# The gate and up products of a hybrid decoder's feed-forward part, as seven half-size block products

## The chip, the cores and the metric

The program runs on one core of a Trainium2 chip, in one launch. The metric is the device time of that launch in microseconds. The engines are called by their names or by the profile's abbreviations: TensorE (PE; its weight loads PEld), VectorE (DVE), ScalarE (ACT), GpSimd (POOL) and SyncE (SP), whose queue issues the loads.

## The reference, cut to what matters

One inference step of a two-layer trunk, on 512 prompt positions and 8 x 4 decode positions, 544 columns in all, with a model width of 1024. Each layer has a mixing half (four head groups) and a feed-forward half. The change is in the feed-forward half:

```python
def hybrid_layer(x, pos, k_pos, st, p):
    ...
    x = x + jnp.concatenate([out_a, out_b, out_c, out_d], axis=-1) @ p['w_out']
    h2 = rmsnorm(x, p['norm2_g'])
    gate, f_conv_new = causal_dwconv(st['f_conv'], h2 @ p['ffn_w_gate'], p['ffn_conv_w'])
    x = x + (jax.nn.silu(gate) * (h2 @ p['ffn_w_up'])) @ p['ffn_w_down']
```

`causal_dwconv` is a causal depthwise convolution of width 3 over positions; the feed-forward width is 2816. All values are float32.

## The kernel before, in words

Channels lie on the partitions: an activation is a tile of 128 channels by 544 positions (`T`), in two halves of 272 (`HT`). The width 1024 is 8 such tiles (`NK`), the feed-forward width 2816 is 22 blocks of 128 (`NF`).

Every product is split in two: `split` (L496) and `xsplit` (L543) make a high part with ScalarE (a copy to fp32r) and a low part with VectorE (the difference). `gemm` (L654) then adds, for each of the k-blocks, the three terms high x high, high x low and low x high, each for both halves, in one PSUM tile. One matmul is 128 x 128 weights by 272 columns.

Weights come from a generator `weights()` (L604) in the order of use. `wload` loads one weight tile into the ring `wr` (two slots) through the SP queue; `wprep` (L633) makes its high part `wh` on ScalarE (L641) and its low part `wl` on VectorE (L643), in rings of three slots each; `wnext` keeps up to three ready and hands out the oldest.

The order of TensorE's instructions is the one in which the program emits them (class `Order` interleaves the side work of the mixing half by due times; the feed-forward half has no side work). The other engines' order is chosen by the framework's scheduler, by order of emission among what is ready.

The feed-forward half of a layer (L1555 to L1609) runs over `FGROUPS`, four groups of 6, 6, 6 and 4 blocks. For each block f of a group: `pgt` is the gate product; two VectorE instructions scale it by `rstd` into `pbf` (L1576, L1577); GpSimd copies the conv state in and out; `conv` (L692) is one ScalarE and two VectorE instructions (`cacc`); ScalarE applies SiLU (`sl`); GpSimd multiplies by `rstd` (L1584); VectorE multiplies by the up product `pup` (L1590) and `split` makes `hdh`, `hdl`. After a group's blocks come 8 down products `pdn` over that group's `hid`, each added to x by VectorE (L1600). The last group of the last layer ends in `finale` (L550, `pdl`), which works half by half. The right-hand sides `xs` of the gate and up products are splits of x times g without `rstd`; `rstd` is made by `Norm.finish` (L526), whose matmuls (`nps`) stand inside the first up product.

PSUM: ring `mm` of two wide tiles (gate, up, down), ring `ps` of two, and the single tiles `pa0` and `pa1`.

## Time and profile before

| what | us |
|---|---|
| median of 3 runs | 1375.87 (1374.64 to 1376.35) |
| the profiled execution | 1375.83 |
| its span, first to last instruction | 1374.0 |
| TensorE busy | 1343.9 |
| VectorE busy | 777.2 |
| ScalarE busy | 515.2 |
| GpSimd busy | 292.2 |

The span is what the profile covers; 1.8 us of the profiled execution's time lie around it. Busy times overlap. The feed-forward half of layer 0 begins at 285.35 us of the span, that of layer 1 at 963.72.

### The profile page before, as it was taken

What the parts mean: (1) busy time and instruction counts of PE and PEld (TensorE: products, weight loads), DVE (VectorE), ACT (ScalarE), POOL (GpSimd) and SP (SyncE); (2) the same over time, 40 slices, a digit from 0 to 9 for tenths busy, and PEclk for the clock granted to TensorE, in tenths of its full rate; (3) what the DMA queues carried; (4) which work ended last, traced back from release to release, by engine and by line L of the source; (5) the groups of instructions that cost most, each with busy time, mean ns of one, the idle gap of its engine ahead of it and who ended that gap; (6) DMA issues with size and microseconds to landing.
All of it is one profiled execution on the core that took longest, in us unless ns stands there. A gap on an engine that the chain in (4) does not pass through costs nothing.

```text
span 1374.0 us, 30046 instructions
## 1 busy us (share of the span) xinstructions
PE 1343.9 (98%) x12982; PEld 1299.8 (95%) x12982; DVE 777.2 (57%) x1319; ACT 515.2 (37%) x852; POOL 292.2 (21%) x466
## 2 busy tenths in 40 slices
PE   8899999999999999999998999999999999999997
PEld 7888888999999999999998888989999999999997
DVE  5897944665445445435658977537444444444446
ACT  5446324443223223313534353335432332232234
POOL 2431220032103102203124311202320230121121
PEclk9899999999999999999999999999999999999999
DMA  6222241232232232232432222413223232322323
GB/s 224 89 83 72 82 133 43 82 113 77 81 106 79 76 107 80 74 106 67 140 120 79 78 82 62 138 52 87 92 81 89 93 85 80 98 89 71 103 68 96
DMA packets 48084, 125.62 MB, mean 91 GB/s; under 512 B 10144, under 2 KB 14432, under 8 KB 47824
## 3 DMA queue, kind: packets, MB, share of 16 engines
q1 hardware_dynamic: 47952, 123.70, 29.6%
q8 instruction: 102, 1.67, 0.5%
q14 instruction: 30, 0.25, 0.1%
HBM read 115.01 MB, written 8.67 MB: 90 GB/s over the span
## 4 chain that ended last, share of the span: by engine, by line
PE 88%; DVE 8%; issue 2%; ACT 1%; DMA 0%; DVEq 0%; SPq 0%; ACTq 0%
PE pup L417 19%; PE pgt L417 19%; PE pdn L417 19%; PE po L417 7%; PE ptm L417 2%; PE pj_b L417 2%; PE pj_z L417 2%; PE pj_u L417 2%; PE pj_h L417 2%; PE pj_cq L417 2%; PE pj_c L417 2%; PE p L417 2%; PE pj_v L417 1%; DVE wl L643 1%; DVE cacc L696 1%
## 5 line engine op out<-in xcount | busy, mean ns | idle before, releaser
L641 ACT ACTIVATE wh<-wr 128x1024 fp32r<-128x1024 f32 (+3 forms) x218 | 208.5, 957 | 502.0 <-PE pdn L417 177.2
L643 DVE TENSOR_TENSOR wl<-wr,wh 128x1024 fp32r<-128x1024 f32 (+3 forms) x218 | 246.2, 1129 | 24.2 <-ACT wh L641 18.3
L417 PE MATMUL pgt<-xl,wh 128*128 128x272 f32 x704 | 146.7, 290 | 0.0
L417 PE MATMUL pup<-xl,wh 128*128 128x272 f32 x704 | 146.7, 290 | 0.0
L417 PE MATMUL pup<-xh,wl 128*128 128x272 f32 x704 | 145.9, 289 | 0.0
L417 PE MATMUL pgt<-xh,wl 128*128 128x272 f32 x704 | 145.9, 289 | 0.0
L417 PE MATMUL pup<-xh,wh 128*128 128x272 f32 x704 | 145.9, 288 | 0.0
L417 PE MATMUL pgt<-xh,wh 128*128 128x272 f32 x704 | 145.9, 288 | 0.0
L417 PE MATMUL pdn<-hdl,wh 128*128 128x272 f32 x688 | 142.8, 289 | 0.0
L417 PE MATMUL pdn<-hdh,wh 128*128 128x272 f32 x688 | 142.4, 288 | 0.0
L417 PE MATMUL pdn<-hdh,wl 128*128 128x272 f32 x688 | 142.2, 288 | 0.0
L1600 DVE TENSOR_TENSOR xr<-xr,pdn 128x544 f32<-128x544 f32 x62 | 44.7, 721 | 142.0 <-PE pdn L417 141.8
L1578 POOL COPY sfo<-pbf 128x2 f32<-128x2 f32 x44 | 14.8, 336 | 517.9 <-DVE pbf L1576 517.9
L1576 DVE TENSOR_TENSOR pbf<-pgt,rstd 128x512 f32<-128x512 f32 x44 | 30.5, 693 | 148.3 <-PE pgt L417 142.9
L417 PEld LDWEIGHTS pgt<-xh,wh 128*128 128x128 f32 x704 | 110.8, 188 | 0.0
L417 PEld LDWEIGHTS pup<-xh,wh 128*128 128x128 f32 x704 | 110.8, 188 | 0.0
L417 PEld LDWEIGHTS pup<-xl,wh 128*128 128x128 f32 x704 | 110.7, 189 | 0.0
L417 PEld LDWEIGHTS pgt<-xl,wh 128*128 128x128 f32 x704 | 110.7, 189 | 0.0
L417 PEld LDWEIGHTS pgt<-xh,wl 128*128 128x128 f32 x704 | 110.7, 188 | 0.0
L417 PEld LDWEIGHTS pup<-xh,wl 128*128 128x128 f32 x704 | 110.7, 188 | 0.0
L417 PEld LDWEIGHTS pdn<-hdl,wh 128*128 128x128 f32 x688 | 108.1, 188 | 0.1
L417 PEld LDWEIGHTS pdn<-hdh,wl 128*128 128x128 f32 x688 | 108.1, 188 | 0.0
(523 smaller groups left out, 2680.0 us busy)
## 6 DMA issues: line engine op xcount, KB each, us to landing
wr<-w_g SPq DMA_DIRECT2D x44, 512.0 KB
wr<-w_u SPq DMA_DIRECT2D x44, 512.0 KB
wr<-w_ch SPq DMA_DIRECT2D x38, 512.0 KB
wr<-w_d SPq DMA_DIRECT2D x48, 384.0 KB
wr<-w_o SPq DMA_DIRECT2D x12, 384.0 KB
wr<-w_d SPq DMA_DIRECT2D x16, 256.0 KB
xr<-x_in SPq DMA_DIRECT2D x7, 544.0 KB
wr<-w_tm SPq DMA_DIRECT2D x8, 392.0 KB
```

The costliest lines, as they stand in the source:

```text
L417: nc.tensor.matmul(out, lhsT, rhs, **kw)
L641: act(hi, r, AF.Copy)
L643: tt(lo, r, hi.bitcast(F32), op=ALU.subtract)
L696: stt(acc[:, 0:out_n], pb[:, j:j + out_n], wcol[:, j:j + 1], acc[:, 0:out_n], op0=ALU.mult, op1=ALU.add)
L1576: tt(pb[:, 2:2 + SEQ], pflat(p, 0, SEQ), rstd[:, 0:SEQ], op=ALU.mult)
L1578: pool.tensor_copy(sfo[:, f, 0:2], pb[:, SEQ:SEQ + 2])
L1600: tt(xk(m), xk(m), pflat(p), op=ALU.add)
```

## The change

For 19 of the 22 blocks the gate and the up product are taken together as one 2 x 2 block product: the weights are [g1 g2; u1 u2], with 1 and 2 for the first and second four k-blocks, the right-hand side is h = x g rstd with its two k-halves (1, 2) and two column halves. Seven products of half size, with sums of weights and of right-hand sides, give the four results.

- `FGROUPS` becomes five groups of 3, 5, 5, 5 and 4 blocks. The first three blocks (`PLAIN`) stay as they were. `FFN_ORDER` puts the 8 down products of a group between the blocks of the next one, two (in the last group three, three and two) after each block but the last; the last group's own stand at the end.
- `Forms.make` makes the right-hand sides, for one pair of k-blocks each time: two scalings by g and `rstd`, four sums, and the high and low parts of seven half-wide forms. It is called twice after block 0 and twice after block 1.
- `wload` puts gate and up weights of such a block in one buffer (`wgu`, one slot, two DMAs); `wsums` makes two more weight tiles on VectorE (`s31` holds g1 + u1 and u2 + u1 in its halves; `s24` holds g1 + u1 + u2 and g2 + g1 + u1 + u2); `wprep` splits g, s31, s24 and the second half of u.
- `seven` runs the seven chains of 12 matmuls over three PSUM tiles `pA`, `pB`, `pD` and one of the ring `mm` (`pC`), with four copies out of PSUM by ScalarE (`sn`) between chains that go on in the same tile, and VectorE sums for gate and up. The chains use, in this order, g, g, s31, s24, s24, s31, u. No product with `rstd` is left on GpSimd in these blocks.
- The squares' sums of the second norm move from GpSimd to VectorE (`Norm((dve, dve))`).
- Several SBUF pools become one (`slabs`, 51 slots), and a scratch area for DMA is made smaller.

```diff
-FGROUPS = [(0, 6), (6, 12), (12, 18), (18, 22)]
+FGROUPS = [(0, 3), (3, 8), (8, 13), (13, 18), (18, 22)]
+PLAIN = 3
...
+def _ffn_order():
+    o, todo = [], []
+    for f0, f1 in FGROUPS:
+        n = f1 - f0
+        for j, f in enumerate(range(f0, f1)):
+            o.append(("plain" if f < PLAIN else "seven", f, f0, f1))
+            k = -(-len(todo) // max(n - 1 - j, 1))
+            o += todo[:k]
+            todo = todo[k:]
+        o += todo
+        todo = [("down", m, f0, f1) for m in range(NK)]
+    return o + todo
...
+    slabs = ctx.enter_context(tc.tile_pool(name="slabs", bufs=51))
     wrp = ctx.enter_context(tc.tile_pool(name="wrp", bufs=2))
+    wgu = ctx.enter_context(tc.tile_pool(name="wgu", bufs=1))
+    wsp = ctx.enter_context(tc.tile_pool(name="wsp", bufs=2))
     whp = ctx.enter_context(tc.tile_pool(name="whp", bufs=3))
     wlp = ctx.enter_context(tc.tile_pool(name="wlp", bufs=3))
...
-                pool.tensor_tensor(a, a, b, op=ALU.add)
+                self.es[0].tensor_tensor(a, a, b, op=ALU.add)
...
+    class Forms:
+        def __init__(self, src):
+            self.src, self.got, self.b11 = src, [], None
+
+        def make(self, kp):
+            h = []
+            for k in (kp, kp + NK // 2):
+                x, g = self.src(k)
+                t = n5("hn", T)
+                stt(t, x, g, rstd, op0=ALU.mult, op1=ALU.mult)
+                h.append(t)
+            (b11, b12), (b21, b22) = ((t[:, 0:HT], t[:, HT:T]) for t in h)
+            u, v = n5("fu", T), n5("fv", T)
+            n1, n2, t3, n4 = u[:, 0:HT], u[:, HT:T], v[:, 0:HT], v[:, HT:T]
+            tt(n1, b11, b12, op=ALU.subtract)
+            stt(n2, n1, -1.0, b22, op0=ALU.mult, op1=ALU.subtract)
+            tt(t3, b22, b12, op=ALU.subtract)
+            tt(n4, b21, n2, op=ALU.add)
+            j = kp % 2
+            if j == 0:
+                self.b11 = [nx("f1" + c, [128, T], F32R) for c in "hl"]
+            c_ = slice(HT * j, HT * j + HT)
+            act(self.b11[0][:, c_], b11, AF.Copy)
+            tt(self.b11[1][:, c_], b11, self.b11[0][:, c_].bitcast(F32), op=ALU.subtract)
+            sb, su, sv = split(h[1], "f2"), split(u, "f3"), split(v, "f4")
...
+    def chain(o, wt, k0, xs, start=True):
+        hi, lo = wt
+        n = len(xs)
+        for k in range(n):
+            xh, xl = xs[k]
+            for i, (w, x) in enumerate(((hi, xh), (hi, xl), (lo, xh))):
+                mm(o, w[:, k0 + k, :], x, start=start and k == 0 and i == 0, stop=k == n - 1 and i == 2,
+                   skip_group_check=not start)
+            yield 0.0
...
+    def wsums(gu):
+        K = NK // 2
+        g, u = gu[:, 0], gu[:, 1]
+        s31 = wsp.tile([128, NK, 128], F32, tag="ws", name="s31")
+        s24 = wsp.tile([128, NK, 128], F32, tag="ws", name="s24")
+        q = gu.rearrange("p a (h k) f -> p (a h) (k f)", h=2)
+        tt(s31.rearrange("p (h k) f -> p h (k f)", h=2), q[:, 0:4:3], bc(q[:, 2], 1, 2), op=ALU.add)
+        tt(s24[:, 0:K], g[:, 0:K], s31[:, K:NK], op=ALU.add)
+        tt(s24[:, K:NK], g[:, K:NK], s24[:, 0:K], op=ALU.add)
+        return [g, s31, s24, u[:, K:NK]]
...
-            nrm = Norm((pool, pool))
+            nrm = Norm((dve, dve))
...
+            def seven(f):
+                B11, B21, B22, N1, N2, T3, N4 = fm.parts()
+                K = NK // 2
+                a_ = ps("pA", [128, HT])
+                b_ = psa.tile([128, HT], F32, tag="pa1", name="pB")
+                d_ = psa.tile([128, HT], F32, tag="pa0", name="pD")
+                sn = pd.tile([128, 4, HT], F32, tag="d5", name="sn")
+                pb, dec = gate_in(f)
+                n = SEQ - HT
+                wg_ = wnext()
+                yield from chain(a_, wg_, 0, B11)
+                act(sn[:, 0], a_, AF.Copy)
+                yield from chain(b_, wg_, K, B21)
+                tt(pb[:, 2:2 + HT], b_, sn[:, 0], op=ALU.add)
+                w31 = wnext()
+                yield from chain(d_, w31, K, N1)
+                act(sn[:, 1], d_, AF.Copy)
+                w24 = wnext()
+                yield from chain(a_, w24, 0, N2, start=False)
+                act(sn[:, 2], a_, AF.Copy)
+                yield from chain(d_, w24, K, B22, start=False)
+                tt(pb[:, 2 + HT:2 + SEQ], d_[:, 0:n], sn[:, 2, 0:n], op=ALU.add)
+                tt(dec[:, :, 2:6], bs(d_[:, n:HT]), bs(sn[:, 2, n:HT]), op=ALU.add)
+                sl = gate_out(f, pb, dec)
+                yield from chain(a_, w31, 0, T3, start=False)
+                act(sn[:, 3], a_, AF.Copy)
+                up = n5("up", T)
+                stt(up[:, HT:T], a_, -1.0, sn[:, 1], op0=ALU.mult, op1=ALU.subtract)
+                c_ = psmm("pC")[:, 0:HT]
+                yield from chain(c_, wnext(), 0, N4)
+                tt(up[:, 0:HT], c_, sn[:, 3], op=ALU.subtract)
+                tt(sl, sl, up, op=ALU.mult)
+                hid[f] = split(sl, "hd")
+                yield 0.0
+
+            for kind, i, f0, f1 in FFN_ORDER:
+                if kind == "plain":
+                    for step in plain(i, i == 0):
+                        yield step
+                    if i < 2:
+                        fm.make(2 * i)
+                        fm.make(2 * i + 1)
+                    continue
+                if kind == "seven":
+                    yield from seven(i)
+                    continue
...
+                p = psmm("pdn")
+                yield from gemm(p, wnext(), hd)
+                tt(xk(m), xk(m), pflat(p), op=ALU.add)
```

`gate_in` and `gate_out` are the lines of the old loop for the conv state, the convolution and SiLU; `plain` is the old body of a block.

## Rows read from the trace of the kernel before

**Rows 1.** The page: busy time by engine, and the chain that ended last, by engine.

```profile
PE 1343.9 (98%) x12982; PEld 1299.8 (95%) x12982; DVE 777.2 (57%) x1319; ACT 515.2 (37%) x852; POOL 292.2 (21%) x466
...
PE 88%; DVE 8%; issue 2%; ACT 1%; DMA 0%; DVEq 0%; SPq 0%; ACTq 0%
```

**Rows 2.** The chain in order of time: start us, length us, what.

```profile
322.29 6.08 PE pgt L417 x48
...
358.77 36.37 PE pdn L417 x288
...
1308.98 6.05 PE pup L417 x48
...
1357.46 4.53 PE pdl L417 x36
```

**Rows 3.** Windows: length, each engine's busy us, clock, DMA share, GB/s.

```profile
248.00:285.35 37.35, 37.35 (x299) 37.35 (x299) 25.02 (x28) 17.20 (x26) 9.08 (x7) 1.00 0.36 106
...
395.14:468.11 72.97, 72.97 (x579) 72.97 (x578) 35.42 (x47) 24.67 (x36) 20.32 (x30) 1.00 0.28 82
468.11:504.37 36.26, 36.26 (x290) 36.26 (x290) 14.06 (x17) 7.84 (x10) 0.00 (x0) 1.00 0.35 96
```

**Rows 4.** VectorE's groups by shape, 395.14 to 468.11: busy us, mean ns, idle before.

```profile
L643 DVE TENSOR_TENSOR wl<-wr,wh 128x1024 fp32r<-128x1024 f32 x10 | 12.3, 1226 | 0.6
L696 DVE SCALAR_TENSOR_TENSOR cacc<-pbf,prm,cacc 128x560 f32<-128x560 f32 x12 | 9.6, 799 | 0.2
L1576 DVE TENSOR_TENSOR pbf<-pgt,rstd 128x512 f32<-128x512 f32 x6 | 4.2, 693 | 21.3 <-PE pgt L417 21.3
L1590 DVE TENSOR_TENSOR sl<-sl,pup 128x544 f32<-128x544 f32 x5 | 3.6, 723 | 12.7 <-PE pup L417 12.7
L500 DVE TENSOR_TENSOR hdl<-sl,hdh 128x544 fp32r<-128x544 f32 x5 | 3.6, 719 | 0.0
L643 DVE TENSOR_TENSOR wl<-wr,wh 128x768 fp32r<-128x768 f32 x2 | 1.9, 950 | 0.0
L1577 DVE TENSOR_TENSOR pbf<-pgt,rstd 128x32 f32<-128x32 f32 x6 | 1.1, 181 | 0.0
L1600 DVE TENSOR_TENSOR xr<-xr,pdn 128x544 f32<-128x544 f32 x1 | 0.7, 722 | 2.5 <-PE pdn L417 2.5
```

**Rows 5.** Tile views, whole span: count, then ns least, median, most; starts.

```profile
L547 DVE SCALAR_TENSOR_TENSOR xl<-xr,prm,xh x32: 772/784/1886, 5.5 to 965.8; 128x544 fp32r<-128x544 f32 x32
...
L593 DVE TENSOR_TENSOR xr<-xr,pdl x4: 429/434/439, 1359.0 to 1364.6; 128x272 f32<-128x272 f32 x4
```

**Rows 6.** Groups by shape of the whole span (VectorE at 272 columns, ScalarE).

```profile
L577 DVE SCALAR_TENSOR_TENSOR xr<-xr,fng,rstd 128x272 f32<-128x272 f32 x4 | 1.8, 489 | 0.0
...
L641 ACT ACTIVATE wh<-wr 128x1024 fp32r<-128x1024 f32 x132 | 139.6, 1058 | 313.9 <-PE pgt L417 142.1 <-PE pdn L417 63.9 <-PE pup L417 27.3
...
L538 ACT ACTIVATE rstd<-nps,cst 128x272 f32<-128x272 f32 x4 | 1.7, 485 | 4.7 <-PE nps L417 4.7
```

**Rows 7.** Timeline of ScalarE, VectorE and SP's queue: start us, length us.

```profile
295.77 0.66 ACT L541 ACTIVATE rstd<-rstd 128x544 f32<-128x544 f32 x1
...
408.23 1.23 DVE L643 TENSOR_TENSOR wl<-wr,wh 128x1024 fp32r<-128x1024 f32 x1
...
409.37 0.72 DVE L500 TENSOR_TENSOR hdl<-sl,hdh 128x544 fp32r<-128x544 f32 x1
...
409.48 0.33 SPq L630 DMA_DIRECT2D wr<-w_g  x1
```

**Rows 8.** Windows behind that load (columns as in rows 3).

```profile
410.50:412.50 2.00, 2.00 (x18) 2.00 (x17) 0.00 (x0) 0.00 (x0) 0.00 (x0) 1.00 0.70 252
412.50:413.50 1.00, 1.00 (x10) 1.00 (x10) 0.08 (x1) 0.33 (x1) 0.00 (x0) 1.00 0.00 0
```

**Rows 9.** Timeline of TensorE: its longest wait ahead of an instruction.

```profile
54.26 1.04 PE L417 MATMUL pe<-gg,cst 128*128 128x16 f32 x4 [4.33 <-DVE gg L765]
```

**Rows 10.** Windows behind it (columns as in rows 3).

```profile
54.00:56.00 2.00, 1.74 (x9) 1.74 (x9) 1.94 (x7) 0.74 (x1) 0.33 (x3) 0.50 0.01 4
...
62.00:64.00 2.00, 2.00 (x15) 2.00 (x15) 1.33 (x3) 1.20 (x2) 1.22 (x2) 0.75 0.00 0
```

More of the change, by code (lines that the diff above doesn't have):

```diff
@@ L451, in n5, with nx @@
         return p5.tile([128, w], F32, tag="w5", name=nm)
-    def nx(nm, shape):
-        return px.tile(shape, F32, tag="x5", name=nm)
+    def nx(nm, shape, dt=F32):
+        return slabs.tile(shape, dt, tag="s5", name=nm)
     def ncc(nm, shape):
@@ L459, in ny @@
     def ny(nm, shape):
-        return pyy.tile(shape, F32, tag="y5", name=nm)
+        return nx(nm, shape)
     def ps(nm, shape):
@@ L615, in weights @@
                 yield I["w_o3"][l, m], NK, 128
-            for f0, f1 in FGROUPS:
-                for f in range(f0, f1):
-                    yield I["w_g"][l, f], NK, 128
-                    yield I["w_u"][l, f], NK, 128
-                for m in range(NK):
-                    yield I["w_d"][l, m, :, f0:f1], f1 - f0, 128
+            for kind, i, f0, f1 in FFN_ORDER:
+                if kind == "down":
+                    yield I["w_d"][l, i, :, f0:f1], f1 - f0, 128
+                elif kind == "plain":
+                    yield I["w_g"][l, i], NK, 128
+                    yield I["w_u"][l, i], NK, 128
+                else:
+                    yield I["w_g"][l, i], I["w_u"][l, i]
     wgen = weights()
-    wload_, wready = [], []
+    wload_, wsplit_, wready = [], [], []
     def wload():
         x = next(wgen, None)
-        if x is not None:
+        if x is None:
+            return
+        if len(x) == 3:
             r = wrp.tile([128, x[1], x[2]], F32, tag="wr", name="wr")
             nc.sync.dma_start(r, x[0])
-            wload_.append(r)
-    def wprep():
-        if not wload_:
-            wload()
-        if not wload_:
-            return
-        r = wload_.pop(0)
+        else:
+            r = wgu.tile([128, 2, NK, 128], F32, tag="wg", name="wg")
+            for i, src in enumerate(x):
+                nc.sync.dma_start(r[:, i], src)
+        wload_.append(r)
+    def wsums(gu):
[8 more added lines that the diff above has]
+        return [g, s31, s24, u[:, K:NK]]
+    def wprep():
+        if not wsplit_:
+            if not wload_:
+                wload()
+            if not wload_:
+                return
+            r = wload_.pop(0)
+            wsplit_.extend([r] if len(r.shape) == 3 else wsums(r))
+        r = wsplit_.pop(0)
         nk, w = r.shape[1], r.shape[2]
@@ L786, in gates @@
         L.beta, L.nbeta, L.gg, L.ex, L.bec = beta, nbeta, gg, ex, bec
[L787 removed]
+        L.oT = [nx(f"oT{pr}", [128, T]) for pr in range(2)]
         od.mark(f"gates{l}", 1.0)
     def halves(x):
[L792 to L793 removed]
+        h, lo = nx("hvh", [128, SEQ], F32R), nx("hvl", [128, SEQ], F32R)
         act(h, x, AF.Copy)
@@ new lines, in main, with gate_in, gate_out @@
+            hid = {}
+            fm = Forms(lambda k: (xk(k), P(l, "n2g", k, k + 1)))
+            def gate_in(f):
+                pb = n5("pbf")
+                return pb, conv_in(pb, 3, stf[:, f])
+            def gate_out(f, pb, dec):
+                pool.tensor_copy(sfo[:, f, 0:2], pb[:, SEQ:SEQ + 2])
+                pool.tensor_copy(sfo[:, f, 2:18].rearrange("p (b s) -> p b s", b=DB), dec[:, :, 4:6])
+                acc, accd = conv(pb, 3, P(l, "fcw", 3 * f, 3 * f + 3), 560)
+                sl = n5("sl", T)
+                act(sl[:, 0:SEQ], acc[:, 0:SEQ], AF.Silu)
+                act(bs(sl[:, SEQ:T]), accd, AF.Silu)
+                return sl
@@ new lines, in plain @@
+            def plain(f, first):
+                p = psmm("pgt")
+                yield from gemm(p, wnext(), xs)
+                pu = psmm("pup")
+                gu = gemm(pu, wnext(), xs)
+                if first:
+                    for _ in range(4):
+                        yield next(gu)
+                    nrm.finish()
+                pb, dec = gate_in(f)
+                tt(pb[:, 2:2 + SEQ], pflat(p, 0, SEQ), rstd[:, 0:SEQ], op=ALU.mult)
+                tt(dec[:, :, 2:6], bs(pflat(p, SEQ, T)), bs(rstd[:, SEQ:T]), op=ALU.mult)
+                sl = gate_out(f, pb, dec)
+                pool.tensor_tensor(sl, sl, rstd, op=ALU.mult)
+                yield 0.0
+                yield from gu
+                tt(sl, sl, pflat(pu), op=ALU.mult)
+                hid[f] = split(sl, "hd")
+                yield 0.0
@@ new lines, in main @@
+            for kind, i, f0, f1 in FFN_ORDER:
+                if kind == "plain":
[8 more added lines that the diff above has]
+                    continue
+                m, last = i, f1 == NF
+                hd = [hid[f] for f in range(f0, f1)]
+                if last and l + 1 == depth and m >= NK - 2:
+                    if m == NK - 2:
+                        yield from finale(xk, xr, nnrm, hd)
+                    continue
+                p = psmm("pdn")
+                yield from gemm(p, wnext(), hd)
+                tt(xk(m), xk(m), pflat(p), op=ALU.add)
+                if last:
+                    if l + 1 < depth:
+                        nx_xs.append(xsplit(xk(m), P(l + 1, "n1g", m, m + 1)))
+                    nnrm.feed(m, xk(m))
+                    if l + 1 == depth:
+                        act(xk(m), xk(m), AF.Copy, scale=fng[:, m:m + 1])
+                yield 0.0
```

75 lines of the change are left out of this document (14 added, 61 removed).

## The prediction

> **What bounds the kernel now.** I read the page first: TensorE is busy 98% of the span and carries 88% of the chain that ended last, VectorE 8% [rows 1]. Then the chain in order of time: through both feed-forward parts it is a row of matmul pieces that touch one another. A 48-matmul product takes 6.08 us in layer 0 and 6.05 us in layer 1, eight down products of 36 matmuls 36.37 us [rows 2]. That is 126.7 and 126.0 ns a matmul, and the windows show TensorE busy for the whole of each stretch, VectorE for 35.42 of 72.97 us in a gate/up group and 14.06 of 36.26 us in a down stretch [rows 3]. So in this stage the time is the number of matmuls times 126 ns, and the other engines have room. Third, the groups of VectorE by shape give the price of all that the change hands to it [rows 4 to 6].
>
> **The change part by part.**
>
> *Matmuls removed.* A gate/up pair takes 2 x 8 k-blocks x 3 split terms x 2 halves = 96 matmuls of 272 columns. As seven products of 4 k-blocks x 3 terms it takes 84. 12 fewer x 19 blocks = 228 a layer: 228 x 126.7 + 228 x 126.0 ns = 57.6 us. The new form uses a weight for one half only; the last down products, which already run so, take 4.53 us for 36, 125.8 ns [rows 2], so the pace holds. Down products stay 1056 a layer however they are grouped. (The Trainium skill, "TensorE: Matmul & The Clock Gate", section "Back-to-back issue gap", gives an isolated matmul N/2.4 + 2.5 ns, 115.8 ns for 272 columns; by it the saving would be 52.8 us and the time below 5 us higher. The row is slower than the rule, and the row decides.)
>
> *VectorE, one seven-product block.* Widths without a row lie between their neighbours. Low parts of 3.5 weight tiles in place of 2: 3 x 1.226 + 0.693 = 4.37. Weight sums, 1024 + 512 + 512 wide: 1.226 + 2 x 0.693 = 2.61. Gate sums, 272, 240 and 32 wide: 0.434 + 0.40 + 0.181 = 1.02. Convolution 2 x 0.80 = 1.60. Up differences 0.489 + 0.434 = 0.92. Product and its low part 0.723 + 0.719 = 1.44. Sum 11.96. The eight rows of [rows 4] add up to 37.0 us where the engine was busy 35.42 [rows 3], since neighbours overlap; scaled by 0.957 it is 11.4 us. TensorE needs 84 x 126.5 = 10.6 us. So a seven alone is longer on VectorE than on TensorE; what makes room is the down products between. With two of five blocks (7.6 us on TensorE; low part of 640 columns 0.82 + sum 0.72, twice, 2.9 us scaled) a period is 18.2 against 14.4 us, 79%. In the first group of sevens the downs span three blocks: 10.6 + 4.6 = 15.2 against 11.4 + 2.4 = 13.9 us, 91%. Five groups instead of four add eight sums of 0.722 us a layer, counted in this.
>
> *ScalarE.* Per seven: 3 x 1.06 and about 0.63 for high parts, four copies out of PSUM at 0.485 at most [rows 6], and convolution, SiLU and split as before, some 2.3: about 8 us of 15 to 18. It hides.
>
> *The forms, and where the largest new wait comes.* The seven right-hand sides need x times g times rstd, so nothing of them starts before rstd, which is ready at 295.77 + 0.66 = 296.4 us [rows 7]. The three plain blocks end on TensorE at 322.29 [rows 2]: 25.9 us. One pair of k-blocks costs two scalings 2 x 0.784, three differences or sums 3 x 0.434 and one of 0.489, low parts 0.434 + 3 x 0.719: 5.95 us, four of them 23.8. The first chain needs all but the last pair's three wide low parts: 21.6. In the same stretch VectorE has three gate evictions (3 x 0.874), two convolutions (3.2), two products with split (2.9), low parts of three weight tiles (3.7), and the first block's sums (2.6). Together 36.6, scaled 35.0 us in 25.9: TensorE waits 9.2 us in each layer, 18 in all. Lower bound: packed instructions start sooner, as the 1.23 us one at 408.23 is followed 1.14 later [rows 7], which takes about 3 us off, and small items slip behind the start: 5 a layer. Upper: gaps in which VectorE waits for ScalarE's high parts or for one of six buffers, and a backlog that runs into the 91% group: 15 a layer. I take 18, bounds 10 to 30.
>
> *Two sevens in a row*, at three places a layer (7 and 8, 12 and 13, 17 and 18). One buffer holds gate and up of a block. It comes free when the low part of the up half is made, which waits for the slot of g, released after two chains (3.0 us); with 0.63 + 0.69 us that is about 4.5 us into the block. A 512 KB load was issued at 409.48, right behind the low part that ended at 409.46, and its transfer was over by 412.5, 3.0 us later [rows 7, 8]; the second one adds 1 to 2 us, 4.5 in all, so at 9 the sums can begin. They and the low part of the next g take 2.6 + 1.2 us, scaled 3.6, to 12.6, with the third matmul due at 10.6 + 0.25: a wait of 1.7 us, a little less where a sum starts on the first load alone: 1.5, six times, 9 us. Bounds 0 (all falls into a gap) and 3 each (convolution ahead of the sums): 0 to 18.
>
> *The weight ring.* High and low parts have three slots each. s31 is used by the third and the sixth chain, so its slot frees only at 9.1 us, and the following weight is split into it under the cover of the last chain, 1.5 us: high part 0.75 and low part 0.82 for a down weight of 640 columns. It just fits if VectorE is free; a convolution instruction in progress costs up to 0.8. I take 0.2 us for each of the other 32 blocks, 6 us, bounds 0 to 1.3 each (0 to 42).
>
> *Small parts.* The squares' sums move from POOL to VectorE: seven of 0.72 us a layer beside 25.0 busy of 37.35 us [rows 3]; rstd is fixed by its place among TensorE's matmuls; in return x's low parts, which reach 1886 against 784 ns [rows 5], may shorten. Nothing. POOL's product with rstd goes for 19 blocks: nothing. The last block's split before the final downs, a little later than now: 1 us a layer, 2. The merged pool of 51 slabs, the added loads' order on the SP queue (each load waits behind the two down weights ahead of it, all loaded a period early) and the smaller DMA scratch: no row shows them; -3 to +3, taken as 0.
>
> Sum: -57.6 + 18 + 9 + 6 + 2 = -22.6 us. The profiled execution took 1375.83 (span 1374.0 and 1.8 around it; the median of the runs is 1375.87): 1353 us.
>
> **The rivals.**
>
> *Covered.* VectorE runs the forms packed and catches up within the first seven, and the ring and the pairs cost nothing: 10 + 0 + 3 + 2 = 15 us of waits, 1333 us. For it: VectorE's idle time of 3.6 us before each gate eviction today (21.3 over six) [rows 4] and 79% load in three of five groups. Against: the 25.9 us between rstd and the first seven are overbooked by any count.
>
> *Half clock.* The wait before the first seven comes in one piece. TensorE waited 4.33 us before 54.26 [rows 9], and the granted clock stood at 0.50, the 1.2 GHz level, from 54 on and was back in part at 62 to 64 [rows 10]: 8.7 us at half speed, 4.4 lost. With a wait of 9.2 the same follows in each layer, some 5 us each, so 1363 us. Against: the wait may come in parts under 2 us, at the second and third gate and at the first chains. (The Trainium skill, same page, section "HAM oscillation — how this bites in real kernels": a wait between bursts of matmuls lets the clock fall, and each next burst starts cold. The windows here agree in kind; whether a broken wait counts no row shows.)
>
> *Slower: the ring.* Each seven ends in a wait for the next weight. s31's slot frees 1.5 us before the next weight is due, and then ScalarE's 0.75 to 1.06 and VectorE's 0.82 to 1.23 must both run, with a convolution pair of 1.6 or the 2.6 us of sums in front. At the upper bound of 1.3 us a block: -57.6 + 18 + 2 + 38 x 1.3 = +12, 1388 us. It decides from (57.6 - 20) / 38 = 1.0 us a block on. For it: VectorE is booked 79 to 91%, so it is seldom free when the high part is done. Against: the low part is asked for earlier than the convolution that would stand in its way, and only one 0.8 us instruction can be in progress.
>
> *Not what it says.* If TensorE's pace rose by a seventh with single-use weights the gain would go; the 125.8 ns row speaks against it, and I give it nothing of its own.
>
> **How the numbers follow.** Forecast 1353: 0.47. Covered, 1333: 0.21. Half clock, 1363: 0.11. Ring near its break-even, within 0.2%: 0.05. Ring above it, 1388: 0.16. Faster by over 0.2% (2.75 us, about what a measurement of this kernel tells from no change): 0.47 + 0.21 + 0.11 = 0.79; same 0.05; slower 0.16. Range: down to 1328, where only the forms' lower bound is left, and up to 1382, the middle of the slower case; it leaves out some 0.05 below and 0.1 to 0.15 above.
>
> **What the profile after would show.** Step one is right if a seven holds 84 matmuls at 126 ns; wrong if they stand further apart with nothing waited for. The forms: a hole of about 9 us on TensorE ahead of the first seven of each layer, released by VectorE, with VectorE full from rstd on. The pairs: 1 to 2 us at the start of blocks 8, 13 and 18, released by the low part of g. The ring: gaps of tenths after each seven. VectorE's busy time should rise by 38 x (11.4 - 5.9) + 2 x 22.8 + 16 x 0.72 + 14 x 0.72 = 276 us, 5.9 being a sixth of 35.42 [rows 3]. The prediction is wrong if TensorE waits at every chain for a copy out of PSUM, if gaps per seven reach 1 us, or if the hole before the first seven is missing or twice as long.

## The result and the profile after

The changed kernel takes 1433.81 us (median of four runs, 1430.1 to 1438.92), the kernel before 1375.99 beside it (1374.64 to 1376.35). The ratio is 1.0425, 95% interval [1.0387, 1.0462]: 58 us slower, where 1353 was forecast and 1382 was the top of the range. The profiled execution has a span of 1437.1 us, 1438.9 with what lies around it.

The page of the kernel after: busy time by engine, and the chain that ended last by engine. They answer to [rows 1].

```profile
PE 1316.7 (92%) x12526; PEld 1260.8 (88%) x12526; DVE 1022.0 (71%) x1751; ACT 647.8 (45%) x1128; POOL 188.8 (13%) x412
...
PE 54%; DVE 26%; DMA 8%; issue 6%; ACT 4%; SPq 1%; DVEq 0%; POOL 0%; ACTq 0%
```

The 456 matmuls are gone (12982 to 12526). But TensorE's share of the chain fell from 88% to 54%, VectorE's rose from 8% to 26%, and DMA, which had nothing, holds 8%. So TensorE now stands and waits, for VectorE, and VectorE or the thing behind it waits for loads. TensorE's waits by what released them (total us, times, longest us), again of the kernel after:

```profile
PE pdn L436 <- DVE up L1710: 30.7, 21, 3.4
PE pdn L436 <- DVE xr L1734: 23.9, 8, 3.9
...
PE pup L436 <- DVE sl L1675: 8.0, 4, 3.4
PE pdn L436 <- ACT hdh L516: 7.1, 2, 4.1
PE pA L436 <- ACT sn L1691: 6.3, 6, 1.1
PE pD L436 <- DVE wl L727: 5.3, 6, 1.4
```

The two largest are waits of a down product, 54.6 us together. Neither the forms (`pup` with the 3.9 of a gate product, 11.9) nor the pairs (`pA` and `pD`, 11.6) come near them. Windows of the feed-forward part of layer 0 (columns as in [rows 3]), from its start to the end of the forms' stretch, to the end of the last seven, to its end:

```profile
285.00:330.00 45.00, 39.06 (x296) 38.48 (x295) 38.82 (x62) 22.62 (x36) 11.15 (x12) 0.96 0.12 37
330.00:692.00 362.00, 323.95 (x2478) 318.96 (x2477) 256.23 (x376) 162.33 (x267) 20.54 (x79) 0.98 0.27 85
692.00:717.50 25.50, 25.01 (x177) 24.76 (x178) 18.24 (x26) 14.69 (x23) 3.86 (x4) 0.89 0.45 147
```

Of 432.5 us TensorE is busy for 388.0 and idle for 44.5. At 126.7 ns [rows 2] the 2940 matmuls that are left (3 x 96 + 19 x 84 + 1056) would take 372.5; another 15 us are therefore lost while it is busy. Most of that is a lower clock: one less the granted clock, times the length, gives some 12 us over the three windows, an estimate from their rounded clocks. Twice 60 us a layer less the 57.6 saved is +62, against the profiled run's +63.

Where the idle time lies is seen on the row of weight loads: start, length, what, and in brackets the idle time before it. These are the waits of over 0.4 us in the first group of sevens, and one pair and one later block as samples:

```profile
345.41 0.30 PEld L436 LDWEIGHTS pdn<-hdh,wh 128*128 128x128 f32 x2 [2.85 <-issue]
364.80 0.30 PEld L436 LDWEIGHTS pdn<-hdh,wh 128*128 128x128 f32 x2 [2.76 <-ACT sl L1656]
383.98 0.50 PEld L436 LDWEIGHTS pdn<-hdh,wh 128*128 128x128 f32 x2 [4.07 <-issue]
403.63 0.30 PEld L436 LDWEIGHTS pdn<-hdh,wh 128*128 128x128 f32 x2 [3.10 <-issue]
422.28 0.19 PEld L436 LDWEIGHTS pD<-f3h,wl 128*128 128x128 f32 x1 [1.05 <-DVE wl L727]
424.86 0.28 PEld L436 LDWEIGHTS pA<-f3h,wh 128*128 128x128 f32 x1 [1.27 <-ACT sn L1691]
...
456.95 0.30 PEld L436 LDWEIGHTS pdn<-hdh,wh 128*128 128x128 f32 x2 [1.62 <-ACT wh L725]
```

Such a wait stands ahead of the second down product behind each of the fifteen sevens of layer 0 that have down products behind them; the first down product starts without one. The fifteen come to 31.4 us, the three pairs to 6.8, the stretch of the forms to 6.5 and the last block to 4.3. (Their sum of 49 is over 44.5, because a weight load's idle time begins before that of the matmuls.)

One period shows how the wait arises. The chain of waits of the kernel after (start, length, what), from the first chains of a block to the down product that was late:

```profile
441.26 1.50 PE pA L436 x12
...
444.84 0.70 DVE wl L727
...
445.94 4.38 DMA wg<-w_u
...
456.98 4.01 PE pdn L436 x30
```

And what VectorE did in the same stretch (start, length, line, what, idle before):

```profile
448.89 0.41 DVE L1701 TENSOR_TENSOR pbf<-pD,sn 128x240 f32<-128x240 f32 x1 [3.35 <-PE pD L436]
449.21 0.18 DVE L1702 TENSOR_TENSOR pbf<-pD,sn 128x32 f32<-128x32 f32 x1
449.46 0.82 DVE L727 TENSOR_TENSOR wl<-wr,wh 128x640 fp32r<-128x640 f32 x1
450.41 1.23 DVE L709 TENSOR_TENSOR s<-wg 128x1024 f32<-128x1024 f32 x1
451.55 0.80 DVE L780 SCALAR_TENSOR_TENSOR cacc<-pbf,prm,cacc 128x560 f32<-128x560 f32 x1
452.26 0.82 DVE L727 TENSOR_TENSOR wl<-wr,wh 128x640 fp32r<-128x640 f32 x1
453.00 0.68 DVE L710 TENSOR_TENSOR s<-wg,s 128x512 f32<-128x512 f32 x1
453.60 0.80 DVE L780 SCALAR_TENSOR_TENSOR cacc<-pbf,prm,cacc 128x560 f32<-128x560 f32 x1
454.32 1.22 DVE L727 TENSOR_TENSOR wl<-wg,wh 128x1024 fp32r<-128x1024 f32 x1
455.45 0.68 DVE L711 TENSOR_TENSOR s<-wg,s 128x512 f32<-128x512 f32 x1
456.05 0.43 DVE L1707 SCALAR_TENSOR_TENSOR up<-pA,sn 128x272 f32<-128x272 f32 x1
456.40 0.43 DVE L1710 TENSOR_TENSOR up<-pC,sn 128x272 f32<-128x272 f32 x1
```

The block begins at 441.26. The low part of its own up weights (444.84) keeps the only gate/up buffer until 445.54; then the load of the next block is issued, and it has landed 9.1 us into the block. In the meantime VectorE is idle for 3.35 us. When the gate sums are done, the next block's first sum (L709) stands in its queue ahead of this block's convolution and ahead of the two up differences, and so do L710, the low part of the next g (454.32) and L711. TensorE ends its seven chains at 451.8 and one down product at 455.6. The second down product needs a place in the ring `mm` of two; the one it is due has `pC` in it, which L1710 empties only at 456.85.

Here VectorE hardly waits for the load itself. At five places of layer 0 it does, for 0.5 to 2.1 us, and there the wait of the down product tends to be longer: behind the 1.60 us below it is 3.10 us (497.81), where its neighbours have 1.6.

```profile
491.27 1.23 DVE L709 TENSOR_TENSOR s<-wg 128x1024 f32<-128x1024 f32 x1 [1.60 <-DMA wg<-w_u]
```

The four waits of the first group of sevens, 12.8 of the 31.4 us, are of another place. There the second down product starts before L1710 has emptied `pC`; what releases it is L1734, which adds the first down product to x and so empties that product's own place:

```profile
344.58 0.71 DVE L1734 TENSOR_TENSOR xr<-xr,pdn 128x544 f32<-128x544 f32 x1
345.44 0.49 PE L436 MATMUL pdn<-hdh,wh 128*128 128x272 f32 x2 [2.66 <-DVE xr L1734]
347.30 0.43 DVE L1710 TENSOR_TENSOR up<-pC,sn 128x272 f32<-128x272 f32 x1
```

The first down product, of 18 matmuls here, ends at about 342.8, but L1734 stands in VectorE's queue behind the sums L709 and L710, the convolution and the low part of the next g. So it is the same queue, and the same ring `mm`, by another of its places.

### The profile page after: what moved, and what is told of

Read it like the earlier page. It is cut to its first block, busy times and chain, and to the rows that moved or that the text cites. A ratio compares the mean times of both kernels' runs of the same rounds, so it can differ in the third digit from the quotient of the medians.

```text
span 1437.1 us, 29920 instructions
## 1 busy us (share of the span) xinstructions
PE 1316.7 (92%) x12526; PEld 1260.8 (88%) x12526; DVE 1022.0 (71%) x1751; ACT 647.8 (45%) x1128; POOL 188.8 (13%) x412
## 4 chain that ended last, share of the span: by engine, by line
PE 54%; DVE 26%; DMA 8%; issue 6%; ACT 4%; SPq 1%; DVEq 0%; POOL 0%; ACTq 0%
PE pdn L436 13%; DVE wl L727 7%; PE po L436 7%; DMA wg<-w_u 6%; PE pA L436 6%; DVE cacc L780 5%; PE pB L436 3%; PE pD L436 3%; ACT wh L725 2%; PE pj_b L436 2%; PE ptm L436 2%; PE pj_cq L436 2%; PE pj_z L436 2%; PE pj_h L436 2%; PE pj_c L436 2%
## 5 line engine op out<-in xcount | busy, mean ns | idle before, releaser
L725 ACT ACTIVATE wh<-wr 128x1024 fp32r<-128x1024 f32 (+5 forms) x158 | 131.3, 831 | 151.8 <-PE pD L436 32.5
L436 PEld LDWEIGHTS pdn<-hdh,wh 128*128 128x128 f32 x688 | 113.3, 198 | 68.8 <-ACT wh L725 31.0
L727 DVE TENSOR_TENSOR wl<-wr,wh 128x1024 fp32r<-128x1024 f32 (+5 forms) x158 | 156.3, 989 | 19.2 <-ACT wh L725 17.1
L725 ACT ACTIVATE wh<-s 128x1024 fp32r<-128x1024 f32 x76 | 80.5, 1059 | 95.7 <-PE pdn L436 71.8
L727 DVE TENSOR_TENSOR wl<-s,wh 128x1024 fp32r<-128x1024 f32 x76 | 92.7, 1220 | 4.4 <-ACT wh L725 1.6
L725 ACT ACTIVATE wh<-wg 128x1024 fp32r<-128x1024 f32 x76 | 64.2, 845 | 54.6 <-PE pB L436 30.5
L1734 DVE TENSOR_TENSOR xr<-xr,pdn 128x544 f32<-128x544 f32 x78 | 55.9, 717 | 36.5 <-PE pdn L436 36.4
L727 DVE TENSOR_TENSOR wl<-wg,wh 128x1024 fp32r<-128x1024 f32 x76 | 72.5, 954 | 5.9 <-ACT wh L725 5.1
L780 DVE SCALAR_TENSOR_TENSOR cacc<-pbf,prm,cacc 128x560 f32<-128x560 f32 x88 | 70.0, 796 | 2.2 <-ACT cacc L778 2.0
L709 DVE TENSOR_TENSOR s<-wg 128x1024 f32<-128x1024 f32 x38 | 46.6, 1226 | 15.5 <-DMA wg<-w_u 14.6
L436 PE MATMUL pD<-f3h,wl 128*128 128x272 f32 x152 | 44.5, 293 | 5.3 <-DVE wl L727 5.3
L436 PE MATMUL pA<-f3h,wl 128*128 128x272 f32 x152 | 45.7, 301 | 0.7 <-DVE wl L727 0.7
```

The costliest lines, as they stand in the source:

```text
L436: nc.tensor.matmul(out, lhsT, rhs, **kw)
L709: tt(s31.rearrange("p (h k) f -> p h (k f)", h=2), q[:, 0:4:3], bc(q[:, 2], 1, 2), op=ALU.add)
L725: act(hi, r, AF.Copy)
L727: tt(lo, r, hi.bitcast(F32), op=ALU.subtract)
L780: stt(acc[:, 0:out_n], pb[:, j:j + out_n], wcol[:, j:j + 1], acc[:, 0:out_n], op0=ALU.mult, op1=ALU.add)
L1734: tt(xk(m), xk(m), pflat(p), op=ALU.add)
```

## The experiments

Each was timed beside the kernel before (1374.7 to 1376.0 us). The edits are against the changed kernel unless another is named.

**The order on VectorE alone.** The sums may stand only behind the up difference that empties `pC`; the buffer stays single.

```diff
-                tt(up[:, 0:HT], c_, sn[:, 3], op=ALU.subtract)
+                last_up[0] = tt(up[:, 0:HT], c_, sn[:, 3], op=ALU.subtract)
...
+        if last_up[0] is not None:
+            with tc.issue_after(last_up[0].ins):
+                return wsums_(gu)
```

> One edge added: VectorE's three weight sums of the next block are issued behind the last up difference (the one that frees pC) of the block before. Theory A (order): in the changed kernel those sums wait for the one gate/up buffer's load while convolution and up differences stand behind them in VectorE's queue, and the second down product waits for pC's PSUM slot. Then the gaps of 1.6 to 4.3 us ahead of the second down product after each seven (some 30 us a layer) and the half clock behind them (some 14 us a layer) should mostly go: 1350 to 1365 us. Theory B (amount): VectorE simply has too much to do (1022 us busy, 313 of 432 in the first feed-forward part): the gaps stay in sum, 1420 us or more. Theory C: the late load itself sets the pace, wherever the sums stand: 1400 to 1430.

Measured 1384.51 us, ratio 1.0066 [1.0051, 1.0081]: 49 us of the loss are gone, and not all of it: the time lies between the 1350 to 1365 of theory A and the 1400 to 1430 of theory C. Of the waits before the second down products of layer 0 one of 1.1 us is left. In the first group, where the down products are short, new ones stand at the next block's fourth chain, for the high part of s24 and, 1.0 us more, for its low part (weight load of this kernel):

```profile
368.32 0.19 PEld L436 LDWEIGHTS pA<-f3h,wh 128*128 128x128 f32 x1 [1.65 <-ACT wh L733]
```

Sums made so late make their own block late. The order is one cause; the time at which the load lands sets how good any order can be.

**`pC` in a place of its own, the order as it is.**

```diff
-                c_ = psmm("pC")[:, 0:HT]
+                c_ = ps("pC", [128, HT])
```

> One edit: pC takes a slot of the two-slot ring of pA in place of the down products' ring, and VectorE's order keeps the next block's sums ahead of convolution and up differences. Theory A with the PSUM slot as its second half: the second down product no longer waits for the up difference, so most of the 16 us of such waits a layer goes, but VectorE is still held by the load, so part returns as waits of later down products for their x sums and of the next block for its weights: 1375 to 1405 us. If the PSUM slot alone were the cause: 1355 us or less. Theory B (amount): 1420 or more.

1394.64 us, 1.0136 [1.0119, 1.0153]: 39 us gone, within the expectation. TensorE's wait has moved, from the second down product to the next block's `pA`, which takes the place that the last block's `pA` leaves when the up difference L1707 has emptied it (waits of this kernel):

```profile
PE pA L436 <- DVE up L1707: 35.6, 11, 5.2
```

The waits before the second down products of the first group are gone too: with `pC` elsewhere the ring `mm` serves only the down products there. So a place in `mm` is how VectorE's lateness reaches TensorE at that point; the lateness itself stays.

**An early load.** Two gate/up buffers; four slots of the merged pool pay for it.

```diff
-    slabs = ctx.enter_context(tc.tile_pool(name="slabs", bufs=51))
+    slabs = ctx.enter_context(tc.tile_pool(name="slabs", bufs=47))
-    wgu = ctx.enter_context(tc.tile_pool(name="wgu", bufs=1))
+    wgu = ctx.enter_context(tc.tile_pool(name="wgu", bufs=2))
```

> Two gate/up buffers in place of one (and 47 slabs in place of 51, to make room). The load of the next block then starts a block earlier, and the scheduler puts its sums among the down products. Theory A: no wait for a load is left in VectorE's queue, and also the two-in-a-row places start on time: 1340 to 1360 us. Theory B (amount): 1420 or more, as VectorE does the same work. Theory C (late load): like A, and then clearly below the first run, by 15 us or more.

1350.54 us, 0.9818 [0.9803, 0.9833]: 83 us less than the changed kernel, and 24 below the kernel before; 34 below the first experiment, as theory C asked. The load is now one block ahead, and the scheduler, which orders VectorE by what is ready, puts the sums among the down products, behind the convolution and the up differences. Of the waits before the second down product nothing over 0.3 us is left in layer 0. What is left are the forms (6.5 us), the pairs and the last block:

```profile
407.26 0.19 PEld L436 LDWEIGHTS pA<-f3h,wh 128*128 128x128 f32 x1 [1.01 <-ACT sn L1691]
...
648.02 0.50 PEld L436 LDWEIGHTS pdn<-hdh,wh 128*128 128x128 f32 x2 [3.33 <-ACT hdh L516]
```

This edit changes two things, the load and with it the order. The next run separates them.

**The early load with the old order.** Two buffers, but the next block's sums are put right behind this block's gate sums, and its convolution behind the sums.

```diff
+    def presum():
...
+            pre.append((r, wsums_(r)))
...
-                tt(dec[:, :, 2:6], bs(d_[:, n:HT]), bs(sn[:, 2, n:HT]), op=ALU.add)
-                sl = gate_out(f, pb, dec)
+                d2 = tt(dec[:, :, 2:6], bs(d_[:, n:HT]), bs(sn[:, 2, n:HT]), op=ALU.add)
+                with tc.issue_after(d2.ins):
+                    presum()
+                with tc.issue_after(last_sum[0].ins):
+                    sl = gate_out(f, pb, dec)
```

> Two buffers for gate and up, so that the load is early as in the version with two buffers (1350.5 us), but VectorE's order is forced back to that of the changed kernel: the next block's three weight sums stand behind this block's gate sums and ahead of its convolution and up differences. Theory A, the order harms only by way of the load, because the first sum waits for it with the rest queued behind: with the load early, 1348 to 1358 us. Theory B, the order harms by itself: between the gate sums and the difference that frees pC's place in PSUM there stand then three sums, two low parts of down weights, the convolution and one low part of 1024 columns, some 8 us of VectorE work, against the 7.6 us (two chains and one down product) after which the second down product wants that place; a wait of 1 to 2 us before the second down product of each block, at some 30 blocks with the half clock behind the longer ones: 1375 to 1400 us. Between the two: both, in the share that the time shows.

1390.94 us, 1.011 [1.0093, 1.0127]: theory B. The order harms with the load out of the way; the same loads of weights wait as before, each for less (this kernel):

```profile
345.25 0.30 PEld L436 LDWEIGHTS pdn<-hdh,wh 128*128 128x128 f32 x2 [2.54 <-DVE xr L1757]
364.00 0.30 PEld L436 LDWEIGHTS pdn<-hdh,wh 128*128 128x128 f32 x2 [2.16 <-issue]
...
446.01 0.30 PEld L436 LDWEIGHTS pdn<-hdh,wh 128*128 128x128 f32 x2 [1.17 <-ACT wh L745]
```

In layer 0 the fifteen come to 22.3 us instead of 31.4, and the pairs show nothing over 0.4. The edit is a little stronger than the order it copies: the convolution's steps on ScalarE and GpSimd stand behind the sums too. So the four times bound the two causes rather than divide them exactly:

| | load behind the block's own low parts | load a block ahead |
|---|---|---|
| sums ahead of convolution and up differences | 1433.8 | 1390.9 |
| sums behind them | 1384.5 | 1350.5 |

The order is worth 40 to 49 us, the load 34 to 43, and together they are the 83. The runs of the changed kernel alone spread over 9 us, so each of these sizes is known to a few us only.

**Is the amount of VectorE's work the bound?** To the version with two buffers the first sum of every block is added a second time.

```diff
+        tt(s31.rearrange("p (h k) f -> p h (k f)", h=2), q[:, 0:4:3], bc(q[:, 2], 1, 2), op=ALU.add)
```

> Against the two-buffer kernel (1350.5 us): one more VectorE sum of 1024 columns in each of the 38 blocks (the first sum made a second time, same values), 1.15 to 1.23 us each, 44 to 47 us of VectorE work in all. Theory A (order and the late load, not the amount): VectorE has room for most of it between the downs, but little in the first group of sevens: up to 12 us longer, 1351 to 1363. Theory B (amount): it shows nearly in full: 1385 to 1397.

1363.43 us, 0.9908 [0.9894, 0.9923]. VectorE is busy for 1064.3 us instead of 1021.1, and of these 43 us 13 show. It is a little over the 12 that theory A allowed and far from the 35 to 47 of theory B. The engine has room in most periods; the loss of the changed kernel was not for want of it.

**The down products spread over all blocks of the next group.** In groups of five 2, 2, 2, 1, 1 instead of 2, 2, 2, 2, 0, and in the last group two after each of four instead of 3, 3, 2, 0; with two buffers.

```diff
-            k = -(-len(todo) // max(n - 1 - j, 1))
+            k = -(-len(todo) // (n - j))
```

> Against the two-buffer kernel (1350.5 us) one line changes: the previous group's down products are spread over all blocks of a group, the last one too, so no two sevens stand next to one another and one or two down products stand between the last seven and its own group's downs. If the waits left in that kernel are where its trace puts them (1.0 us at each of three pairs and 3.6 us ahead of the last group's downs, with the half clock behind it, in each layer), some 10 to 15 us go: 1336 to 1342. If VectorE's amount of work sets what is left, nothing changes: 1348 to 1353.

1332.01 us, 0.9678 [0.9662, 0.9695]: 18.5 less than with two buffers alone and the best version measured that computes the whole result, 44 us faster than before. The expectation, 1336 to 1342, was too small a gain. It removes the pairs and the wait of the last block together, since two down products now stand between the last seven and the down products that need it. Its windows of layer 0:

```profile
285.00:330.00 45.00, 39.07 (x287) 38.50 (x286) 38.45 (x60) 21.75 (x34) 10.22 (x11) 0.92 0.12 37
330.00:640.00 310.00, 309.96 (x2470) 309.33 (x2470) 255.36 (x378) 161.73 (x267) 25.00 (x80) 1.00 0.30 98
```

From the first seven to the end of this window at 640 TensorE has next to no idle time and the full clock. What is left to lose is in the 45 us before.

**The same spreading with one buffer and the sums behind.** The line above, on the kernel of the first experiment.

> The first run's edge (sums behind the last up difference, 1384.5 us with one gate/up buffer) together with the spread down products. If the one buffer's late load was left as the cost there, mainly where two sevens meet and where the period is short, the spread takes the pairs away but the short periods of the first group stay: 1345 to 1362. If the order was all: 1332 to 1338, as with two buffers.

1359.08 us, 0.9882 [0.9867, 0.9898], within the expectation: 27 us above the version with two buffers, which is what the late load still costs when the order and the pairs are mended.

**The price of the forms.** On the best version, only the first of four `make` calls is done and its forms are used for all k-blocks; three quarters of the right-hand sides are so left out of the computation.

```diff
-                    if i < 2:
-                        fm.make(2 * i)
-                        fm.make(2 * i + 1)
+                    if i == 0:
+                        fm.make(0)
+                        fm.got *= 4
```

> Against e5_spread (1332.0 us, 6.5 us of waits a layer left, all in the plain blocks): only the first pair's right-hand sides are made and used for all four, so three quarters of the forms' work is left out and the output is not the reference's. If the forms are what those waits come from, they go with the half clock behind them: 1316 to 1320, which is 1375.8 less the 57.6 us of removed matmuls. If something else in the plain blocks holds TensorE: 1328 or more.

1315.65 us, 0.957 [0.9553, 0.9587], at the lower end of the expectation. The window of the forms' stretch has TensorE nearly full:

```profile
285.00:330.00 45.00, 44.45 (x354) 44.26 (x354) 32.09 (x45) 22.08 (x34) 9.91 (x16) 1.00 0.15 43
```

So the three calls left out cost 16.4 us, the fourth leaves half a us of idle time in that window, and 1315.7 is within 3 us of the 1318.2 that the removed matmuls alone would leave.

**The forms: other places, another engine.** Two of the four sums of each form on GpSimd, on the version with two buffers:

```diff
+            pool.tensor_tensor(t3, b22, b12, op=ALU.subtract)
...
-            tt(t3, b22, b12, op=ALU.subtract)
-            tt(n4, b21, n2, op=ALU.add)
+            pool.tensor_tensor(n4, b21, n2, op=ALU.add)
```

> Against the two-buffer kernel (1350.5 us): two of the four sums of each pair of right-hand sides are made by GpSimd. My step on the forms says VectorE is overbooked between rstd and the first seven, and its trace shows 6.5 us of waits a layer there. Eight sums of 0.43 us leave VectorE, so 3.4 us of booked work a layer: 4 to 8 us in all, 1342 to 1347. If GpSimd's slower sums or its hold on shared access lengthen the chain of each pair, nothing or a loss: 1350 to 1358.

1357.32 us, 0.9865 [0.9851, 0.988], 7 us slower than without and not 4 to 8 faster: the other branch of the expectation. The waits before the third gate product and the third up product went from 2.2 and 3.6 to 3.4 and 3.4 us, and others of 1.3 and 1.4 appeared behind them. VectorE has 16 instructions fewer, some 7 us, and yet is busy for 1022.7 us against 1021.1, because others take longer beside the sums on GpSimd. Here a low part beside one of them takes 1.30 us, where the next one (310.73) takes 0.71 (this kernel):

```profile
309.40 0.82 POOL L583 TENSOR_TENSOR fv<-hn 128x272 f32<-128x272 f32 x1 [2.30 <-DVE hn L578]
309.50 1.30 DVE L517 TENSOR_TENSOR f2l<-hn,f2h 128x544 fp32r<-128x544 f32 x1
```

A fourth plain block on the best version, to give the forms more time (`PLAIN = 4`, groups of 4, 5, 5, 4 and 4):

> Against e5_spread: four plain blocks instead of three, groups of 4, 5, 5, 4 and 4. The forms get 12 us more of VectorE's time for 12 matmuls more a layer (1.5 us). If the overbooked stretch before the first seven is what is left (6.5 us of waits and 1 to 2 of half clock a layer), 8 to 12 us less than e5_spread; if something else holds the second and third plain block, 3 us more than it.

1338.27 us, 0.9725 [0.971, 0.9739]: 6 us slower than with three, where 8 to 12 less or 3 more was expected. The waits of 0.74, 2.15 and 3.61 us stay, because `make` is still called behind the first two blocks and its instructions still stand ahead of these blocks' evictions.

With four plain blocks, the calls later (none behind block 0, then one, one and two):

> Against e8_plain4 (1338.3 us; four plain blocks did not help): the forms are made later, pair by pair after blocks 1, 2 and 3, with evictions ahead of them. Now both the order and the amount are eased. If e8 kept its waits because forms stood ahead of evictions: 1321 to 1328, under e5_spread. If not: 1336 to 1341.

1340.71 us, 0.9753 [0.9735, 0.977]: the other branch of the expectation. The early waits are gone and one of 5.58 us stands at the first seven, with two of 1.2 behind it.

With three plain blocks, the calls behind the second and third block:

> Against e5_spread (1332.0 us): the forms are made one plain block later (two pairs after block 1, two after block 2), so that the blocks' own evictions come first on VectorE. If the stretch from rstd to the first seven is overbooked in amount, as my step on the forms says (35 us of work in 26), the wait only moves from the plain blocks to the first seven's chains: 1330 to 1338. If the wait was made by the order alone: 1318 to 1324.

1345.32 us, 0.978 [0.9765, 0.9796], worse than the 1330 to 1338 expected. Nearly all of the waiting has become one wait, at the first seven, and the clock is down around it (weight load, and the window on it, of this kernel):

```profile
334.63 0.29 PEld L436 LDWEIGHTS pA<-f1h,wh 128*128 128x128 f32 x1 [11.55 <-ACT f1h L591]
...
322.00:335.00 13.00, 1.67 (x12) 1.37 (x10) 12.97 (x21) 4.48 (x9) 6.79 (x3) 0.69 0.00 1
```

VectorE is busy for 12.97 of these 13 us. Wherever the calls are put, the wait for the forms is there in some shape: this stretch, unlike the rest, is bound by the amount of work.

## Why the prediction was wrong, and where it was right

**The saving was right.** 456 matmuls at the old pace: a chain of 12 takes 1.50 us (the `pA` piece at 441.26), 125 ns each, though each weight is used for one half only. 1375.8 - 57.6 = 1318.2, and the run without most of the forms took 1315.7.

**The forms were right in size, and came in the shape that was named as possible.** Forecast 18 us, measured 16.4 for three of the four calls. They came not as one hole before the first seven but as waits of 0.7, 2.2 and 3.6 us at the second up product and at the gate and up products behind it, whose evictions stood behind form instructions on VectorE; the first seven began without a wait. So the rival with the half clock behind one long hole did not come about at that place, but in part it did: in the best version the 48 matmuls behind the 3.60 us take 8.91 us instead of 6.08 [rows 2].

**VectorE's load was a little too high**: it rose by 245 us, to 1022, where a rise of 276 was forecast.

**The pairs were of the right order, at another place**: 2.1 to 2.4 us each, 14 us in all (twice layer 0) where 9 stood in the sum, inside its bounds of 0 to 18. The wait was forecast at the start of the second seven, for the low part of its g. It came at its third and fourth chain, for the low part of s31 and for ScalarE's copy of `pA`, which stood behind the high parts of s24 and of the up weights. Of this 1.0 us each stayed with the early load.

**The last block was too low**: 4.3 us in layer 0 instead of 1.

**The step that failed is the weight ring, the term of 6 us for what TensorE waits behind each seven.** "I take 0.2 us for each of the other 32 blocks" was said of a wait for the next weight's low part, and against the slower rival it was held that "the low part is asked for earlier than the convolution that would stand in its way, and only one 0.8 us instruction can be in progress". Measured in layer 0: 31.4 us, which is 1.96 us for each of the 16 blocks a layer that the term counts, beyond its bound of 1.3, and up to 4.07 at one place; in the two layers TensorE's two rows of such waits come to 54.6 us where 6 stood in the sum. Over all nineteen sevens it is 1.65 each, beyond the 1.0 from which that rival decided and the 1 us that the prediction itself named as a sign of being wrong. Three things were wrong in it.

- *What TensorE waits for.* The prediction looked at the next weight. The first down product behind a seven, which uses that weight, began without a wait. The wait is for a place in PSUM: `pC` shares the ring `mm` with the down products, so the second of two down products waits at eleven of the fifteen places for the up difference L1710, and at the four of the first group, 12.8 us, for the sum L1734 that empties the place of the first. Everything that VectorE has queued ahead of these two counts.
- *What stands ahead of it.* The load was timed to a tenth: 4.5 us to the release, 4.5 for the load, sums from 9 us on; measured 4.3, 4.4 and 9.1. But this was priced only where two sevens meet. With one buffer the sums become ready about then in the other blocks too, when the gate sums are done and the convolution is not, and there they were put. From 450.41 on VectorE works without a pause for 6.4 us before `pC` is empty, and L709, L710, L711 and the low part of the next g are 3.5 us of it by the spacing of their starts; the wait was 1.6. In the runs, putting the sums behind took 49 us off, moving `pC` 39, and loading a block ahead with the order kept 43.
- *What the waits bring with them.* A wait at each block was priced at its own length. Behind four of the fifteen the down product ran in part at the lower clock, which costs some 7 us of layer 0 by the granted clocks of the windows there; the rest of the 15 us lies behind the forms' waits, the first pair and the last block, or is not accounted for.

The rival "slower: the ring" had the right side and a kindred mechanism, VectorE's queue, at the wrong place and too low a price (1388). The averages over a period, 79 and 91% booked, did not tell the cost: with the same work in another order and the early load the waits were gone, and the extra sum added to that version shows that room was left there. Once load and order are mended, 1350.5 us stands where the prediction had 1353; this agreement is in part chance, since its terms for pairs, ring and last block differ from what that run shows. (The rival "covered" says that the ring and the pairs cost nothing and adds 3 us for them; nothing hangs on it.)

What stays open: how the 83 us divide between order and load more closely than 40 to 49 and 34 to 43, and whether another form of the plain stretch could hide the 16 us of the forms. Four arrangements were tried for the latter and none did.

## What to carry to other kernels

When work is handed to an engine that runs its queue in order, its booked share does not tell the cost: find out when each new instruction becomes ready, which instruction stands behind it, and which PSUM place or buffer that one frees for the engine you want to keep busy. A single buffer whose load can start only within the current block makes work ready in the middle of that block, which is where it does harm; a second buffer (83 us here) or an order written out (49 us) is worth trying before the idea itself is dropped. And if side work lies between the blocks of a group, leave none of them without it, the last one too (18.5 us).

## What the runs showed of the hardware

**Waits of 2.5 to 3.1 us were followed by the lower clock at some places and not at others.** [rows 9, 10] had it behind one of 4.33 us. In the kernel after, the stretch behind the 2.85 us wait at 345.41 has a granted clock of 0.61 (the last column but two), between the levels of 1.2 and 2.4 GHz; 18 matmuls of the down product take 3.75 us there, 208 ns each, and the clock is largely back in the second stretch. Behind the waits of 2.76 us at 364.80 and of 3.10 us at 497.81 (third and fourth stretch) it stays at 1.00:

```profile
345.50:349.00 3.50, 3.50 (x19) 3.50 (x20) 2.96 (x5) 0.17 (x1) 0.00 (x0) 0.61 0.00 0
349.00:352.00 3.00, 3.00 (x23) 3.00 (x23) 2.55 (x3) 1.84 (x3) 0.00 (x0) 0.89 0.00 0
...
364.90:368.40 3.50, 3.50 (x28) 3.50 (x29) 2.77 (x5) 1.21 (x2) 0.00 (x0) 1.00 0.00 0
...
497.90:501.40 3.50, 3.50 (x28) 3.50 (x29) 2.71 (x4) 0.66 (x1) 0.00 (x0) 1.00 0.00 0
```

Behind another wait of 3.10 us, at 403.63, it was 0.59 over the next 3.5 us, so the length of the wait alone does not decide. Behind the 1.62 us wait at 456.95 it stays at 1.00. In the run with the old order and the early load it was 0.61 behind 2.54 us and 1.00 behind 2.16. (The Trainium skill, "TensorE: Matmul & The Clock Gate", section "HAM oscillation — how this bites in real kernels", describes a kernel in which each wait between bursts of matmuls makes the next burst start cold. The windows agree in part: the clock fell anew behind four of the fifteen waits of layer 0, but not behind each of the longer ones.)

**VectorE's scalings for the forms take longer beside a GpSimd product.** In the stretch of the forms of the kernel after two scalings take 2.59 us while GpSimd multiplies the first block by `rstd`; one alone takes 0.77:

```profile
300.57 2.59 DVE L578 SCALAR_TENSOR_TENSOR hn<-xr,prm,rstd 128x544 f32<-128x544 f32 x2
300.94 1.64 POOL L1672 TENSOR_TENSOR sl<-sl,rstd 128x544 f32<-128x544 f32 x1 [3.60 <-ACT sl L1656]
...
304.42 0.77 DVE L578 SCALAR_TENSOR_TENSOR hn<-xr,prm,rstd 128x544 f32<-128x544 f32 x1
```

That is 1.05 us more than two of them alone, and a second such pair beside a GpSimd product takes 2.57 (317.47). (The Trainium skill, "SBUF — State Buffer", section "Who interferes with whom", says that a VectorE instruction with two SBUF inputs and a GpSimd instruction that reads SBUF hold each other up whole. The stretched pairs agree, and so do the stretched low parts in the run with two sums on GpSimd. How much of that run's 7 us comes from it was not measured on its own.)
